# Four edits to the order and the blocks of a fused Hymba layer on one NeuronCore: norm matmuls moved, first weights in halves, bias matmuls moved, end in token blocks of 400, 400 and 256

## The chip, the core and the metric

The kernel runs on one core of one Trainium2 chip. The metric is the device time of one execution in microseconds (us); lower is better. Engines are named as in the profile: PE (TensorE matmul), PEld (its weight load), DVE (VectorE), ACT (ScalarE), POOL (GpSimd), SP (the queue that issues most transfers). Each engine runs its own instructions strictly in the order of the program that was built for it, and waits where an operand is not there yet.

## The reference, cut to what matters

One step of a hybrid streaming encoder: 16 meta tokens, 1024 prompt tokens and 32 sample tokens, 1072 columns in all, model width 1024.

```python
h = rmsnorm(x, norm_mix); z = h @ w_in          # 1024 -> 1792: GLU, q, k, v
a = silu(layernorm(depthwise_conv31(glu)))      # conv group
o = sliding-window attention with sinks and a relative-position bias
x = x + concat([a, o]) @ w_out
u = rmsnorm(x, norm_ffn) @ w_up                 # 1024 -> 2 * 2816
x = x + (silu(depthwise_conv3(gate)) * up) @ w_down
y = rmsnorm(x, norm_final)
```

The meta tokens give no output row of `y`, so the end of the program works on 1056 columns.

## The kernel before, in words

**Layout.** Features lie on the 128 partitions, tokens along the free axis; width 1024 is eight tiles `k` (or `m`) of 128. Almost every product is made three times for accuracy (`mm3`, lines 237 to 242): operands are split into a rounded part and a remainder (`hi`, `lo`), and PE adds hi·hi, lo·hi and hi·lo (lines 240, 241, 242). The split costs one ACT instruction (rounding) and one DVE instruction (subtraction) for every operand. A group below means all matmuls that fill one accumulator; with eight `k` it has 24.

**Order.** In most regions the order of PE (and of ACT and DVE in some) is the order in which the Python code is written (`manual_schedule`). The other engines' order is set by the builder's own scheduler. In the region of the first feed-forward groups (from line 1314) only PE is ordered by hand.

**Start.** PE first runs 18 dummy products (`warm`, line 292). Line 297 loads the weights of the first two output tiles (`raw`, 512 KB each) on SP and splits them; then `xT` comes in twelve pieces of two `k` each (line 299), for three token blocks of 336, 384 and 352 columns (`TB`). `gsplit` (line 273) makes `hi` on ACT and `lo` on DVE for every `k`; `sq_sum` (line 266) squares on ACT and adds up on DVE for the norm. The first PE groups (`START`) take two output tiles against block 0, `k` by `k`, then one tile each against blocks 1 and 2.

**A norm** (`rms_steps`, line 244) has three steps. One: PE sums the squares over partitions (`R<-ones`, line 252: per sub-block of up to 128 tokens one matmul with one column), DVE line 253, POOL line 254 (a power of -0.5) and DVE lines 255 to 257 (one Newton step). Two: ACT makes one diagonal matrix `diag` for each sub-block (line 260). Three: PE multiplies it by ones (`R<-diag`, line 263), which spreads the factors over all partitions. Each `next()` on the generator emits one step.

**Bias setup** (`bias_setup`, line 380) has five steps too; the fourth is two matmuls `nb` (line 424) that read tiles `acc<-ld` which came by DMA, the fifth is `sb` and `mb` (lines 436, 439). `BS` lists the group (input tile number, token block) after which each step is emitted.

**Feed-forward start** (lines 1314 to 1363). The norm of the last token block (`last_rms`, line 1316) is made between the groups of the first feed-forward tile: `group(f, u, p, c)` has 24 matmuls of 266 or 264 columns, u = 0 the gate half, u = 1 the up half. Beside them `t_stage` (line 1215) builds sums and differences of activation blocks for a Strassen-like scheme: ACT `hraw` (line 1224), four DVE operations (1226 to 1229), ACT `th` and DVE `tl` (`hilo`, lines 1135, 1136). `gate_done(0)` (line 1249) needs the finished norm; the weights of tile 1 are split into the buffers of tile 0 (`w_plain`, lines 1135 and 1136 again), the second set into the buffers that the four u = 1 groups free.

**End** (lines 1467 to 1512). The last six of 22 products of the down projection are done block by block in the order 384, 352, 320 columns (`EO`, `YB`). Each of eight `m` takes 18 matmuls, a DVE add into `x` (line 1498), a square on ACT and a sum on POOL. `final` makes the norm of a finished block while the next block's products run: eight DVE operations (line 1477), and stores `yT` on SP. After the third block this tail has nothing beside it.

Of the kernel before, what the change touches and what calls it, by code (L numbers as in the profile page):

```python
# [17 lines left out]
P = 128  # L18
# [42 lines left out]
SQP = (8, 8, 7)  # L61
SQG = (8, 8, 8)
FS = 1
EO = (1, 2, 0)
EM = 5
LNW = (4, 3, 9, 6, 11, 3, 11)
# [91 lines left out]
def body(nc, tc, cp, wp, xp, dp, io):  # L158
# [27 lines left out]
    nc.vector.memset(stat, 1.0)  # L186
    mhalf = cp.tile([P, 3], F32, tag="mhalf", name="mhalf")
    nc.vector.memset(mhalf, -0.5)
# [55 lines left out]
    def rms_steps(sums, c, div, R):  # L244
        parts = sums if isinstance(sums, list) else [sums]
        n = parts[0].shape[-1]
        subs = (0, P, n - P)
        ss = R[:, 400:403]
        v, t, r = (stat[:, c + 3 * i:c + 3 * i + 3] for i in range(3))
# [4 lines left out]
        nc.gpsimd.tensor_tensor(out=r, in0=v, in1=mhalf, op=ALU.pow)  # L254
# [4 lines left out]
        for i in range(3):  # L259
# [16 lines left out]

    diag = [cp.tile([P, P], F32, tag=f"diag{i}", name=f"diag{i}") for i in range(3)]

# [16 lines left out]
    for b, (t0, n) in enumerate(TB):  # L295
        if b == 0:
            pre = [wload(d.win[c].rearrange("p a b -> p (a b)")) for c in range(2)]
        for k in range(0, KD, 2):
            nc.sync.dma_start(X[b][:, k:k + 2, :], d.xT[:, k:k + 2, t0:t0 + n])
        if b == 0:  # L300
            nc.scalar.dma_start(ident, d.cst[:, 0, :])
# [818 lines left out]
    with tc.tile_pool(name="psB", bufs=1, space=PSUM, reuse_waits="tile") as pf:  # L1120
# [295 lines left out]

        def d_mm(ps, ci, w, b):
            t0, n = YB[b]
            f0, f1 = CHUNKS[ci]
# [25 lines left out]
        for i, (ci, m) in enumerate(order[:2 * KD]):  # L1445
# [4 lines left out]
            for b in (1, 2, 0):  # L1450
                ps = mmt()[:, :YB[b][1]]
                d_mm(ps, ci, w, b)
                if ci == 0:
# [12 lines left out]

        def final(pos, b, parts):
            t0, n = YB[b]
            rms = rms_steps(parts, 27 + (pos % 2) * 9, D, pf.tile([P, 512], F32, tag="nm", name="R", bufs=2))
# [5 lines left out]
            w = 2 if pos < 2 else 1  # L1475
            for k in range(KD):
                nc.vector.scalar_tensor_tensor(out=XY(b, k), in0=XY(b, k), scalar=pcol("g3", k), in1=R,  # L1477
                                               op0=ALU.mult, op1=ALU.mult)
                if (k + 1) % w == 0:
                    nc.sync.dma_start(d.yT[:, k + 1 - w:k + 1, t0 - NMETA:t0 - NMETA + n],  # L1480
                                      X[b][:, k + 1 - w:k + 1, t0 - OB[b][0]:])
                if k % 2:
                    yield

        scrs = [z[:, i:i + 384] for z in (rbg, gx0) for i in (0, 384)]
        fin = None
# [3 lines left out]
        ends[3] = d_load(2, 3)  # L1490
        for pos, b in enumerate(EO):
            n = YB[b][1]
            for m in range(KD):
                if not pos and m + 4 < KD:
                    ends[m + 4] = d_load(2, m + 4)
                ps = mmt()[:, :n]
                d_mm(ps, 2, ends[m], b)
                nc.vector.tensor_tensor(out=XY(b, m), in0=XY(b, m), in1=ps, op=ALU.add)
                if m == 0:
                    parts = [rb[b][:, :n]]  # L1500
                if m < SQP[pos]:
                    sq_sum(XY(b, m), rb[b][:, :n], scr(n), m, nc.gpsimd if m < SQG[pos] else nc.vector)
                else:
                    parts.append(scr(n))
                    nc.scalar.activation(parts[-1], XY(b, m), AF.Square)
# [4 lines left out]
            fin = final(pos, b, parts)  # L1510
        for _ in fin:
# [95 lines left out]
```

## Time and profile before

| what | us |
|---|---|
| three runs | 1096.98, 1099.25, 1099.38 |
| median of the runs | 1099.25 |
| the profiled execution, its own time | 1095.78 |
| its span, first to last instruction | 1093.7 |
| PE busy in the span | 1060.2 |

The profiled execution lies 3.5 us under the median of the three runs, so durations read from it are set against 1095.78, and a difference is then taken over to the median. From 376 to 1080 us PE has no idle time that the profile shows, with the exception of 0.02 us near 820. Its idle time lies in the first 9 us, in the attention stretch from 180 to 260 us, in single places between 300 and 376 us, and in the last 13 us.

### The profile page before, as it was taken

To read this page: it belongs to the slowest core of one execution; us is meant where nothing else is said; L and a number is where in the kernel's file an instruction comes from. 1 tells how busy PE (TensorE), PEld (TensorE's weight loads), DVE (VectorE), ACT (ScalarE), POOL (GpSimd) and SP (SyncE) were. 2 spreads that over 40 slices of the span, in tenths; PEclk is the share of its full clock that TensorE was granted. 3 is DMA by queue.
4 is the path that set the end of the run, shared out by engine and by line. 5 is a ranking of instruction groups with operands and counts; after the bars stand their busy time and mean duration, and the time that the engine had idled before them with its cause. 6 is when DMAs were issued, how large, how long until landed. Compare 5 with 4: busy or idle time off the path is not lost.

```text
span 1093.7 us, 18848 instructions
## 1 busy us (share of the span) xinstructions
PE 1060.2 (97%) x7547; PEld 1033.7 (95%) x7547; DVE 775.0 (71%) x1321; ACT 468.6 (43%) x990; POOL 138.3 (13%) x189
## 2 busy tenths in 40 slices
PE   8999999989999699999999999999999999999996
PEld 7989997758999699999999999999999999999996
DVE  7799999999887778777778778777777203322244
ACT  8522227996766754334334334334344213111211
POOL 1111000012334100000000000000001111000231
PEclk9999999999999899999999999999999999999997
DMA  7344331125853111221221221221266746121012
GB/s 263 80 108 100 83 94 40 39 59 82 159 147 124 50 60 59 97 80 60 92 86 59 86 91 60 82 94 60 79 236 202 184 90 159 58 63 59 15 58 101
DMA packets 45823, 103.76 MB, mean 95 GB/s; under 512 B 7840, under 2 KB 25496, under 8 KB 45736
## 3 DMA queue, kind: packets, MB, share of 16 engines
q1 hardware_dynamic: 35912, 84.46, 23.4%
q0 software_dynamic: 9536, 17.89, 9.9%
q8 instruction: 59, 0.97, 0.4%
q14 instruction: 28, 0.23, 0.1%
q10 hardware_dynamic: 288, 0.22, 0.1%
HBM read 72.41 MB, written 21.02 MB: 85 GB/s over the span
## 4 chain that ended last, share of the span: by engine, by line
PE 65%; ACT 2%; DVE 1%; issue 1%; POOL 0%; POOLq 0%; DVEq 0%; ACTq 0%
PE mm L1204 38%; PE mm L240 9%; PE mm L241 9%; PE mm L242 9%; ACT hraw L1224 1%; PE R L263 0%; POOL rb L271 0%; DVE x L1477 0%; ACT bh L274 0%; DVE tl L1136 0%; ACT th L1135 0%; ACT acc L270 0%; ACT diag L260 0%; DVE x L1082 0%; DVE traw L1226 0%
## 5 line engine op out<-in xcount | busy, mean ns | idle before, releaser
L357 DVE SCALAR_TENSOR_TENSOR acc<-glu,prm,acc 128x1090 f32<-128x1090 f32 (+3 forms) x180 | 168.0, 967 | 0.4
L1204 PE MATMUL mm<-bh,sl 128*128 128x266 f32 (+1 forms) x544 | 117.5, 285 | 0.0
L240 PE MATMUL mm<-hi,whi 128*128 128x352 f32 (+3 forms) x312 | 104.5, 335 | 2.0 <-ACT hi L274 2.0
L241 PE MATMUL mm<-lo,whi 128*128 128x352 f32 (+3 forms) x312 | 102.2, 327 | 0.7 <-DVE lo L275 0.7
L242 PE MATMUL mm<-hi,wlo 128*128 128x352 f32 (+3 forms) x312 | 101.8, 326 | 0.0
L1204 PEld LDWEIGHTS mm<-bh,sl 128*128 128x128 f32 x544 | 90.7, 189 | 0.0
L1204 PE MATMUL mm<-th,sl 128*128 128x264 f32 (+1 forms) x384 | 90.2, 285 | 0.0
L1204 PE MATMUL mm<-bl,sl 128*128 128x266 f32 (+1 forms) x296 | 84.5, 285 | 0.0
L1204 PE MATMUL mm<-bh,whi 128*128 128x266 f32 (+1 forms) x320 | 80.9, 285 | 0.0
L240 PE MATMUL mm<-bh,whi 128*128 128x266 f32 (+4 forms) x224 | 68.2, 304 | 0.0
L241 PE MATMUL mm<-bl,whi 128*128 128x266 f32 (+4 forms) x224 | 67.7, 302 | 0.0
L242 PE MATMUL mm<-bh,wlo 128*128 128x266 f32 (+4 forms) x224 | 67.7, 302 | 0.0
L1204 PEld LDWEIGHTS mm<-th,sl 128*128 128x128 f32 x384 | 66.2, 188 | 0.0
L1204 PE MATMUL mm<-th,wlo 128*128 128x266 f32 (+1 forms) x240 | 65.3, 285 | 0.0
L240 PEld LDWEIGHTS mm<-hi,whi 128*128 128x128 f32 x312 | 58.9, 189 | 3.3 <-ACT hi L274 2.2
L241 PEld LDWEIGHTS mm<-lo,whi 128*128 128x128 f32 x312 | 59.1, 189 | 2.2 <-DVE lo L275 1.9
L242 PEld LDWEIGHTS mm<-hi,wlo 128*128 128x128 f32 x312 | 59.0, 189 | 0.0
L1204 PEld LDWEIGHTS mm<-bh,whi 128*128 128x128 f32 x320 | 57.1, 189 | 0.0
L1204 PEld LDWEIGHTS mm<-bl,sl 128*128 128x128 f32 x296 | 55.8, 188 | 0.0
L1204 PE MATMUL mm<-bh,wlo 128*128 128x266 f32 (+1 forms) x208 | 51.7, 284 | 0.0
L1204 PE MATMUL mm<-th,rawr 128*128 128x266 f32 (+1 forms) x208 | 49.1, 285 | 0.0
L1204 PE MATMUL mm<-bh,rawr 128*128 128x266 f32 (+1 forms) x208 | 49.0, 285 | 0.0
(374 smaller groups left out, 3234.3 us busy)
## 6 DMA issues: line engine op xcount, KB each, us to landing
x<-wup SPq DMA_DIRECT2D x40, 512.0 KB, 3.9
wlo<-raw POOLq DMA_DIRECT2D x16, 512.0 KB, 4.5
raw<-wdn SPq DMA_DIRECT2D x16, 512.0 KB, 6.6
raw<-win SPq DMA_DIRECT2D x14, 512.0 KB, 3.4
yd<-x SPq DMA_DIRECT2D x12, 528.0 KB, 2.9
yd<-rb SPq DMA_DIRECT2D x10, 528.0 KB, 3.0
rb<-yd SPq DMA_DIRECT2D x8, 528.0 KB, 5.1
x<-yd SPq DMA_DIRECT2D x7, 528.0 KB, 5.6
```

The lines of the kernel that those rows point to most:

```text
L240: nc.tensor.matmul(ps, whi(k), xhi(k), start=first and i == 0, stop=False)
L241: nc.tensor.matmul(ps, whi(k), xlo(k), start=False, stop=False)
L242: nc.tensor.matmul(ps, wlo(k), xhi(k), start=False, stop=last and i == n - 1)
L357: nc.vector.scalar_tensor_tensor(out=a, in0=e[:, a0 + k:a1 + k], scalar=pcol("cw", p * CW + k), in1=a, op0=ALU.mult, op1=ALU.add)
L1204: nc.tensor.matmul(ps, w[:, j, :], x, start=first and j + i == 0, stop=j == 3 and i == 2, skip_group_check=True)
L1224: nc.scalar.activation(h[:, 2 * i * n + lo_:2 * i * n + hi_], src, AF.Copy, scale=pcol("g2", k))
```

## The change

1. `last_rms`: its first step is emitted after the second group of u = 0 (before: after the third), its second after the third (before: fourth), its third after the first group of u = 1 (before: at once after the fourth group of u = 0).
2. The first two weight tiles come in halves of four `k`, each of 256 KB, two halves ahead of `x` 0 to 3 and two ahead of `x` 4 to 7, and are split half by half.
3. `BS`: steps four and five of the bias setup are emitted one group later.
4. The end works on blocks of 400, 400 and 256 columns that no longer coincide with the stored blocks of `x`; an add, a square, a final multiplication or a store that crosses a border is done in two pieces. `rms_steps` takes as many sub-blocks as the width needs (four for 400, two for 256). All squares run on ACT and all sums but the last on POOL, as before.

```diff
-BS = ((1, 0), (1, 1), (1, 2), (2, 0))
+BS = ((1, 0), (1, 1), (2, 0), (2, 1))
-EO = (1, 2, 0)
+ENDN = 400
+ENDS = ((NMETA + 256, ENDN), (NMETA + 656, ENDN), (NMETA, 256))
...
-        subs = (0, P, n - P)
+        subs = list(range(0, n - P, P)) + [n - P]
...
-            pre = [wload(d.win[c].rearrange("p a b -> p (a b)")) for c in range(2)]
+            pre = [[wp.tile([P, 1024], F32 if t == "raw" else F32R, tag=t, name=t) for t in ("raw", "whi", "wlo")]
+                   for c in range(2)]
         for k in range(0, KD, 2):
+            if b == 0 and k % 4 == 0:
+                for c in range(2):
+                    raw, hi, lo = (z[:, k * P:k * P + 512] for z in pre[c])
+                    nc.sync.dma_start(raw, d.win[c, :, k:k + 4].rearrange("p a b -> p (a b)"))
+                    split(hi, lo, raw)
             nc.sync.dma_start(X[b][:, k:k + 2, :], d.xT[:, k:k + 2, t0:t0 + n])
...
             group(0, 0, i // 2, i % 2)
-            if i > 1:
+            if 0 < i < 3:
                 next(last_rms)
             next(t0s)
-        next(last_rms)
-        gate_done(0)
         w_plain(1, 0, *plain[:2])
         for i in range(4):
             group(0, 1, i // 2, i % 2)
+            if i == 0:
+                next(last_rms)
+                gate_done(0)
             next(t1s)
...
             for k in range(KD):
-                nc.vector.scalar_tensor_tensor(out=XY(b, k), in0=XY(b, k), scalar=pcol("g3", k), in1=R,
-                                               op0=ALU.mult, op1=ALU.mult)
+                for lo_, hi_, x in x_cols(k, t0, n):
+                    nc.vector.scalar_tensor_tensor(out=x, in0=x, scalar=pcol("g3", k), in1=R[:, lo_:hi_],
+                                                   op0=ALU.mult, op1=ALU.mult)
```

The order of DVE around the last block's norm (`stat` are the norm's small operations, `traw`, `rb`, `tl` and `t` belong to `t_stage`), before:

```order
L1227 TENSOR_TENSOR traw<-hraw_3618,traw 128x266
L1136 TENSOR_TENSOR tl_3611<-traw,th_3609 128x3x266
L1226 TENSOR_TENSOR traw<-hraw_3619 128x266
L1228 TENSOR_TENSOR traw<-hraw_3619 128x266
L1229 TENSOR_TENSOR rb<-hraw_3618,traw 128x266
L253 TENSOR_SCALAR stat<-R 128x3
L1227 TENSOR_TENSOR traw<-hraw_3619,traw 128x266
L1229 TENSOR_TENSOR rb<-hraw_3619,traw 128x266
L255 SCALAR_TENSOR_TENSOR stat<-stat 128x3
```

The same place of DVE after (line numbers of the changed kernel, up to eight away):

```order
L1234 TENSOR_TENSOR traw<-hraw_3625,traw 128x266
L1236 TENSOR_TENSOR rb<-hraw_3625,traw 128x266
L252 TENSOR_SCALAR stat<-R 128x3
L1143 TENSOR_TENSOR tl_3618<-traw,th_3616 128x3x266
L254 SCALAR_TENSOR_TENSOR stat<-stat 128x3
L1233 TENSOR_TENSOR traw<-hraw_3626 128x266
L1235 TENSOR_TENSOR traw<-hraw_3626 128x266
L255 TENSOR_TENSOR stat<-stat 128x3
L1234 TENSOR_TENSOR traw<-hraw_3626,traw 128x266
L256 SCALAR_TENSOR_TENSOR stat<-stat 128x3
L1236 TENSOR_TENSOR rb<-hraw_3626,traw 128x266
```

The first `stat` operation and one `rb` operation have moved ahead of a `tl` operation; what stands before them on DVE is the same.

The order of ACT at the same place, where the diagonal matrices are made, before:

```order
L1330 COPY gx_3613<-mm 128x264
L1224 ACTIVATE hraw_3618<-x_2244,prm 128x176
L1224 ACTIVATE hraw_3618<-x_2245,prm 128x352
L1135 CAST th_3609<-traw 128x3x266
L1224 ACTIVATE hraw_3619<-x_2244,prm 128x176
L1224 ACTIVATE hraw_3619<-x_2245,prm 128x352
L260 ACTIVATE diag_93<-ident,stat 128x128
```

And after:

```order
L1231 ACTIVATE hraw_3626<-x_2251,prm 128x176
L1231 ACTIVATE hraw_3626<-x_2252,prm 128x352
L1142 CAST th_3616<-traw 128x3x266
L259 ACTIVATE diag_93<-ident,stat 128x128
L259 ACTIVATE diag_94<-ident,stat 128x128
L259 ACTIVATE diag_95<-ident,stat 128x128
L1337 COPY gx_3620<-mm 128x264
```

One accumulator copy (`gx`) and two `hraw` operations that stood ahead of the `diag` operations now follow them; the `th` operation still stands ahead of them.

The order of ACT at the start of the program, after (before, one row `CAST whi<-raw 128x1024 x2` stood in the place of the first of these, and the second cast row was not there):

```order
L232 CAST whi<-raw 128x512 x2
L273 ACTIVATE hi_79<-xs_103,prm 128x336 x2
L267 ACTIVATE acc<-xs_103 128x336
L269 ACTIVATE sq<-xs_103 128x336
L273 ACTIVATE hi_79<-xs_103,prm 128x336 x2
L269 ACTIVATE sq<-xs_103 128x336 x2
L232 CAST whi<-raw 128x512 x2
L273 ACTIVATE hi_79<-xs_103,prm 128x336 x2
```

The second halves' casts stand between the pieces of `x`; on DVE the second halves' subtractions stand at the corresponding place.

## Rows read from the trace of the kernel before

**Rows 1.** The page, busy time, share of the span and instruction counts.

```profile
PE 1060.2 (97%) x7547; PEld 1033.7 (95%) x7547; DVE 775.0 (71%) x1321; ACT 468.6 (43%) x990; POOL 138.3 (13%) x189
```

**Rows 2.** Waits of PE, whole span: us in total, times, longest us.

```profile
PE R L263 <- ACT diag L260: 10.6, 2, 8.3
...
PE mm L240 <- ACT hi L274: 2.0, 1, 2.0
```

**Rows 3.** Timeline of PE, feed-forward start: start, us, what, [idle before <-releaser].

```profile
360.88 0.72 PE L252 MATMUL R<-ones,rb 128*128 128x1 f32 x6
...
364.35 0.28 PE L242 MATMUL mm<-bh,wlo 128*128 128x264 f32 x1
372.98 1.65 PE L263 MATMUL R<-diag,ones 128*128 128x128 f32 x6 [8.35 <-ACT diag L260]
374.28 0.57 PE L240 MATMUL mm<-bh,whi 128*128 128x266 f32 x1
...
392.94 0.28 PE L242 MATMUL mm<-bh,wlo 128*128 128x264 f32 x1
```

**Rows 4.** Timeline of DVE, the same stretch.

```profile
365.95 0.43 DVE L1227 TENSOR_TENSOR traw<-hraw,traw 128x266 f32<-128x266 f32 x1
367.49 0.99 DVE L1136 TENSOR_TENSOR tl<-traw,th 128x798 fp32r<-128x798 f32 x1 [1.12 <-ACT th L1135]
...
369.21 0.43 DVE L1229 TENSOR_TENSOR rb<-hraw,traw 128x266 f32<-128x266 f32 x1
369.56 0.15 DVE L253 TENSOR_SCALAR stat<-R 128x3 f32<-128x3 f32 x1
...
388.95 1.22 DVE L1136 TENSOR_TENSOR wlo<-raw,whi 128x1024 fp32r<-128x1024 f32 x1
```

**Rows 5.** Timeline of ACT, the same stretch.

```profile
370.97 0.84 ACT L1135 CAST th<-traw 128x798 fp32r<-128x798 f32 x1
372.54 0.97 ACT L260 ACTIVATE diag<-ident,stat 128x128 f32<-128x128 f32 x3
...
386.93 1.05 ACT L1135 CAST whi<-raw 128x1024 fp32r<-128x1024 f32 x1 [0.61 <-PE mm L241]
```

**Rows 6.** Timelines of SP, ACT, DVE and PE in the first 26 us.

```profile
8.04 0.37 SPq L299 DMA_DIRECT2D xs<-xT  x1
8.82 0.37 SPq L299 DMA_DIRECT2D xs<-xT  x1
...
6.49 1.04 ACT L209 CAST whi<-raw 128x1024 fp32r<-128x1024 f32 x1 [1.02 <-DMA raw<-win]
8.12 1.04 ACT L274 ACTIVATE hi<-xs,prm 128x336 fp32r<-128x336 f32 x2 [0.58 <-DMA xs<-xT]
...
8.72 1.05 DVE L275 SCALAR_TENSOR_TENSOR lo<-xs,prm,hi 128x336 fp32r<-128x336 f32 x2
...
25.03 0.43 PE L241 MATMUL o<-lo,whi 128*128 128x352 f32 x1 [0.21 <-DVE lo L275]
```

**Rows 7.** Timeline of PE around the bias matmuls.

```profile
65.01 1.74 PE L424 MATMUL nb<-acc,glu 128*128 128x448 f32 x4 [0.96 <-DMA acc<-ld]
...
70.30 0.76 PE L436 MATMUL sb<-acc,glu 128*128 128x354 f32 x2
```

**Rows 8.** Timelines of PE and DVE after the last product, and one group of DVE operations by form.

```profile
1082.20 0.36 PE L252 MATMUL R<-ones,rb 128*128 128x1 f32 x2
1082.43 0.46 PE L252 MATMUL R<-ones,rbg 128*128 128x1 f32 x2
1085.16 1.65 PE L263 MATMUL R<-diag,ones 128*128 128x128 f32 x6 [2.28 <-ACT diag L260]
...
1086.85 3.76 DVE L1477 SCALAR_TENSOR_TENSOR x<-x,prm,R 128x320 f32<-128x320 f32 x8 [2.24 <-PE R L263]
...
L1477 DVE SCALAR_TENSOR_TENSOR x<-x,prm,R 128x384 f32<-128x384 f32 x8 | 4.5, 608 | 0.0
```

**Rows 9.** Transfers, whole span: issue, engine, count, KB each, median us to landing.

```profile
cap<-glu SPq DMA_DIRECT2D x4, 15.0 KB, 2.9
```

More of the change, by code (lines that the diff above doesn't have):

```diff
@@ L186, in body @@
     nc.vector.memset(stat, 1.0)
-    mhalf = cp.tile([P, 3], F32, tag="mhalf", name="mhalf")
+    mhalf = cp.tile([P, 4], F32, tag="mhalf", name="mhalf")
     nc.vector.memset(mhalf, -0.5)
@@ L246, in rms_steps @@
         n = parts[0].shape[-1]
-        subs = (0, P, n - P)
-        ss = R[:, 400:403]
-        v, t, r = (stat[:, c + 3 * i:c + 3 * i + 3] for i in range(3))
+        subs = list(range(0, n - P, P)) + [n - P]
+        ns = len(subs)
+        ss = R[:, 400:400 + ns]
+        v, t, r = (stat[:, c + ns * i:c + ns * i + ns] for i in range(3))
         for i, at in enumerate(subs):
@@ L258, in rms_steps @@
         yield
-        for i in range(3):
+        for i in range(ns):
             nc.scalar.activation(diag[i], ident, AF.Copy, scale=r[:, i:i + 1])
@@ L275, in gsplit @@
         nc.vector.scalar_tensor_tensor(out=lo, in0=x, scalar=g, in1=hi.bitcast(F32), op0=ALU.mult, op1=ALU.subtract)
-    diag = [cp.tile([P, P], F32, tag=f"diag{i}", name=f"diag{i}") for i in range(3)]
+    diag = [cp.tile([P, P], F32, tag=f"diag{i}", name=f"diag{i}") for i in range(4)]
     cPS = tc.tile_pool(name="psA", bufs=1, space=PSUM, reuse_waits="tile")
@@ L296, in body @@
         if b == 0:
-            pre = [wload(d.win[c].rearrange("p a b -> p (a b)")) for c in range(2)]
+            pre = [[wp.tile([P, 1024], F32 if t == "raw" else F32R, tag=t, name=t) for t in ("raw", "whi", "wlo")]
+                   for c in range(2)]
         for k in range(0, KD, 2):
+            if b == 0 and k % 4 == 0:
[3 more added lines that the diff above has]
+                    split(hi, lo, raw)
             nc.sync.dma_start(X[b][:, k:k + 2, :], d.xT[:, k:k + 2, t0:t0 + n])
+        if b == 0:
+            pre = [z[1:] for z in pre]
         if b == 0:
@@ L1415, in d_load, with d_mm @@
             return kv(hi[:, :w]), kv(lo[:, :w])
-        def d_mm(ps, ci, w, b):
-            t0, n = YB[b]
+        def d_mm(ps, ci, w, t0, n):
             f0, f1 = CHUNKS[ci]
@@ L1451, in body @@
                 ps = mmt()[:, :YB[b][1]]
-                d_mm(ps, ci, w, b)
+                d_mm(ps, ci, w, *YB[b])
                 if ci == 0:
@@ L1465, in body, with final @@
         region.__exit__(None, None, None)
-        def final(pos, b, parts):
-            t0, n = YB[b]
-            rms = rms_steps(parts, 27 + (pos % 2) * 9, D, pf.tile([P, 512], F32, tag="nm", name="R", bufs=2))
+        def final(pos, parts):
+            t0, n = ENDS[pos]
+            rms = rms_steps(parts, (pos % 2) * 12, D, pf.tile([P, 512], F32, tag="nm", name="R", bufs=2))
             for _ in range(2):
@@ L1490, in body @@
         ends[3] = d_load(2, 3)
-        for pos, b in enumerate(EO):
-            n = YB[b][1]
+        for pos, (t0, n) in enumerate(ENDS):
+            last = pos + 1 == len(ENDS)
             for m in range(KD):
@@ L1496, in body @@
                 ps = mmt()[:, :n]
-                d_mm(ps, 2, ends[m], b)
-                nc.vector.tensor_tensor(out=XY(b, m), in0=XY(b, m), in1=ps, op=ALU.add)
+                d_mm(ps, 2, ends[m], t0, n)
                 if m == 0:
[L1500 to L1505, printed above, removed]
+                    parts = [rbt[:, t0:t0 + n]]
+                to = parts[0] if m == 0 else scr(n)
+                for lo_, hi_, x in x_cols(m, t0, n):
+                    nc.vector.tensor_tensor(out=x, in0=x, in1=ps[:, lo_:hi_], op=ALU.add)
+                    nc.scalar.activation(to[:, lo_:hi_], x, AF.Square)
+                if 0 < m < KD - last:
+                    nc.gpsimd.tensor_tensor(out=parts[0], in0=parts[0], in1=to, op=ALU.add)
+                elif m:
+                    parts.append(to)
                 if pos and m >= FS:
@@ L1509, in body @@
                 pass
-            fin = final(pos, b, parts)
+            fin = final(pos, parts)
         for _ in fin:
```

13 lines of the change are left out of this document (5 added, 8 removed).

## The prediction, made before the run

> **What bounds the kernel now.** Read the page's busy shares first: PE works 97% of the span [rows 1]. So a saving counts only where PE stands still, or where the program ends without it. The waits of PE name those places [rows 2]: 10.6 us in two waits for the diagonal matrices of a norm, 8.3 of them in one, and 2.0 us for the first `hi` operand. The timeline adds 0.96 us before the bias matmuls [rows 7]. The large wait stands in the feed-forward start: PE ends its fourth group at 364.5 and starts `R<-diag` at 372.98 [rows 3]. The second wait for `diag`, 2.28 us, is in the tail, which no product covers: DVE's last eight multiplications start at 1086.85 and end at 1090.61 [rows 8], and the span ends at 1093.7.
>
> **Edit 1, the norm in the feed-forward start.** Why was `diag` so late? PE had its column sums at 360.88 plus 0.72 [rows 3], but DVE took them up only at 369.56, behind a `tl` and an `rb` operation [rows 4]; ACT then ran a cast at 370.97 before `diag` at 372.54 [rows 5]. So the delay lies in two queues, not in the matmuls' place alone. The edit moves three things. The column sums come one group earlier on PE, which gains nothing by itself, since DVE was the late one. DVE's first operation moves from behind the `tl` of 367.49 to behind an `rb` that can follow the operation of 365.95 at once [rows 4]: about 366.8, 2.8 us earlier. But on ACT `diag` still stands behind the cast of 370.97; only a copy and two `hraw` operations move behind it. That cast is fed by the same alternation of DVE and ACT as before, so `diag` starts at about 371.6 (370.97 and 0.84, less a copy moved behind) instead of 372.54, and PE gets it at about 372.1. On the other side PE now runs one more group first. A group lasts 3.0 us (from the end of the sums, about 361.5, to 364.35 and 0.12), so PE arrives at about 367.9, some 0.4 of it a wait for the sum on POOL. The wait shrinks from 8.35 to about 4.2, it does not vanish.
>
> If PE then ran free, the third product of the third group of tile 1, which stands at 392.94 [rows 3], would come at 372.1 + (392.94 - 372.98) - 3.0 = 389.1: a gain of 3.9. What is late next is its operand: this product is the first that reads the second `wlo` of tile 1, which DVE made at 388.95 to 390.15 [rows 4]. I walked the 32 DVE rows between with the durations of before and with ACT's copies of the norm now behind one copy more: the `wlo` starts at about 388.5, nearly where it was, since DVE's amount of work up to it is the same. So PE waits there for some 0.6 us, and the place gives 392.94 - 389.7 = **3.2**. Bounds: if the gate chain, which starts only after the norm's copies, slips by 2 us more, 1.2; if DVE is 1 us ahead of my walk, 3.9. PE also ran at half speed after the long wait: 0.57 for the first product at 374.28 against 0.28 [rows 3]. If the shorter wait spares PE that slow time, about 1.5 us, PE only arrives earlier at the same `wlo`; at most, with DVE ahead as well, 5.4.
>
> **Edit 2, the weights in halves.** The first `hi` waited for the first piece of `x`, which landed at 8.04 (SP's issue is released by it; the piece after came 0.78 later) [rows 6]. 512 KB less stand in front of it. At the rate between these two pieces of 336 KB (0.43 MB per us) that is 1.2 us; at the rate between the second weight tile, landed by 6.49, and the first piece, 2.4 us. PE's dummy products end 2.04 us before its first real one, so PE itself could use up to 2.0. But the work of splitting is not less, it now stands between the pieces of `x`: on ACT two casts of half of 1.04 each [rows 6], on DVE two subtractions of half of 1.22 (the same operation as at 388.95 [rows 4]). DVE is what PE follows there: `lo` starts at 8.72, and PE waits for a `lo` as late as 25.03 [rows 6]. DVE's stream starts earlier by 1.2 to 2.1 and has 1.2 to 1.3 more to do from there on, so the stretch ends 0 to 0.9 earlier. I take **0.5**, near the middle; PE then waits 1 us or more at the fifth `k` where it waited at the first. A page of the Trainium skill speaks against this edit: "DMA: Bandwidth & Descriptors", section "Bandwidth", advises transfers of 1 MiB or more, since each carries a fixed share. By its fixed share of about 2.0 us per transfer, if none overlapped, the first piece of `x` would land later than now and the edit would cost about 0.7. The pieces landing 0.78 apart [rows 6] show that transfers overlap here, so the sum does not use that.
>
> **Edit 3, the bias matmuls.** PE waits 0.96 before `nb` for a transfer, and the `sb` group follows one group, 4 us, later without a wait [rows 7]. One group later the transfer has 3.7 us more; ACT's copies and DVE's bias operations have no reader for tens of us. Gain **0.95**, bounds 0.3 (if DVE, which is nearly full there, gives half of it back later) and 1.2.
>
> **Edit 4, the end.** The columns are 1056 in both, the products 144 for each block in both, so the products cost the same. The four-part norms of the two wide blocks add one column-sum pair and one `R<-diag` pair to PE each, amid its products: four pairs at up to 0.24 (0.72 for three [rows 3]), taken as 0.2, costs **0.8**. The split adds, squares and stores on DVE, ACT and SP lie beside 18 products of over 0.1 us each and cost nothing unless DVE fills up: in the third block eight small pieces come on top of work that left DVE idle most of the time. The tail shrinks from 320 columns in three sub-blocks to 256 in two: two column-sum pairs, 0.23 (from 1082.20 to 1082.43) each, 0.46; one pair of `R<-diag`, 1.65/3 = 0.55; eight multiplications, each shorter by the slope between 608 ns at 384 columns and 543 at 320 (4.5/8 against 3.76/8 gives the same, 1 ns a column), 0.065 times 8 = 0.52; add and square together 0.12. Sum **1.65**. Bounds 1.0 (if SP's issues of about 0.4 each bind in place of DVE) and 2.1 (if the smaller stores land faster too).
>
> **Sum.** 3.2 + 0.5 + 0.95 - 0.8 + 1.65 = 5.5. Against the profiled execution, 1095.78 - 5.5 = 1090.3; the median of the runs lies 3.5 above that execution, so 1099.25 - 5.5 = **1093.7**.
>
> **Rivals.**
> (a) *The wait moves down the DVE queue.* The norm's copies stand later on ACT, so the gate chain on DVE slips and `wlo` with it; edit 1 gives 1.2 or less, the sum 2.0 to 3.4, time about 1096.4. For it: DVE is in order and PE already reads `wlo` 2.8 us after it is made [rows 3, 4], so every us beyond that is a wait. Against it: DVE's total work up to that row is unchanged. Chance 0.2.
> (b) *PE runs free.* DVE is ahead of my walk and the clock stays up: edit 1 gives 5 and the sum is 7.3, time about 1091.9. Chance 0.15.
> (c) *The early gains are lost* in the attention stretch where PE waits for other engines: edits 2 and 3 give nothing, 1099.25 - 4.05 = 1095.2. Against it: DVE, which is full there, itself waits for PE before, so it would start that stretch earlier. Chance 0.07.
> (d) *Slower: the narrow stores hold the end.* The stores of 64 and 48 columns, eight of them, go on SP's queue ahead of the last block's eight. The nearest row, a store of 15 KB in short runs, lands in 2.9 us [rows 9]. The last narrow store is issued about 5 us before the first final one. It must take more than 5 + 5.5 = 10.5 us to make the program slower at all, and 14 for 0.3%. Chance 0.03. The same page's section "Specifications" asks for 512 bytes or more in one run, and below that an extra read; these runs have 256 and 192 bytes, and no run here shows a store of this form yet.
> The forecast as summed keeps 0.55.
>
> **Chances.** About 0.3% (3.3 us) is what a measurement of this kernel can tell from no change. Faster by more than that: the forecast, (b), (c), and a quarter of (a): 0.82. Within it: the rest of (a), 0.15. Slower: (d), 0.03. The range 1090.0 to 1097.0 takes in (a) to (c) with their bounds, with the spread of the three runs on either side.
>
> **What would show it.** In the changed profile: the wait before `R<-diag` near 370 at about 4 us (right) or near 8 (wrong), with `diag` on ACT behind the cast; a short new wait near 388 for `wlo` (a longer one is rival (a), none is (b)); the wait for the first `hi` gone and one of 1 us or more at the fifth `k`; no wait before `nb`; six `R<-diag` records in the tail reduced to four, and the time from the last product to the end at about 11.7 instead of 13.3. The prediction is wrong if DVE's `wlo` comes after 392 or if the last stores land more than 4 us after the last multiplication.

## The result: 0.67% faster than before, 1090.7 us

The changed kernel took 1090.66 us, the median of four runs (1090.1 to 1091.2); the kernel before took 1098.12 in four runs beside it. The ratio is 0.9933, with an interval of 0.9915 to 0.9951. When both were run again (below), the ratio was 0.9944 (0.9931 to 0.9956), with the kernel before at 1096.64. The forecast was 1093.7 in a range of 1090.0 to 1097.0, and a gain of 5.5 us. The whole gain is 7.5 us in the first comparison and 6.1 in the second, so its size was near, but not for all of the reasons given: one of the four edits costs time.

The page of the changed kernel and its waits of PE (us in total, times, longest), for [rows 1] and [rows 2]:

```profile
PE 1062.2 (98%) x7549; PEld 1035.2 (95%) x7549; DVE 777.3 (71%) x1355; ACT 471.9 (43%) x1009; POOL 144.9 (13%) x189
```

```profile
PE R L262 <- ACT diag L259: 5.1, 2, 3.0
...
PE mm L238 <- DVE x L1089: 1.9, 2, 1.6
PE mm L239 <- DVE lo L274: 1.5, 3, 0.7
```

The two waits for `diag` fell from 10.6 to 5.1, and the large one among them from 8.3 to 3.0. The wait for the first `hi` (2.0) and the one before `nb` (0.96) are gone. In their place stand longer waits for `lo` at the start (1.5 for 0.7; 0.65 of it at the fifth `k`, where 1 us or more was forecast) and for a DVE result near 313 us (two waits, 1.9 for 1.3).

The feed-forward start after, for [rows 3 to 5]: timelines of PE, then DVE, then ACT (start, us, what, [idle before <-releaser]).

```profile
367.93 0.28 PE L240 MATMUL mm<-bh,wlo 128*128 128x266 f32 x1
371.19 1.65 PE L262 MATMUL R<-diag,ones 128*128 128x128 f32 x6 [2.98 <-ACT diag L259]
372.49 0.57 PE L238 MATMUL mm<-bh,whi 128*128 128x266 f32 x1
...
388.27 0.29 PE L239 MATMUL mm<-bl,whi 128*128 128x264 f32 x1
388.68 0.39 PE L240 MATMUL mm<-bh,wlo 128*128 128x264 f32 x1
```

```profile
366.93 0.15 DVE L252 TENSOR_SCALAR stat<-R 128x3 f32<-128x3 f32 x1
...
386.23 1.25 DVE L1268 TENSOR_TENSOR x<-x,rbg 128x1058 f32<-128x1058 f32 x1
387.40 1.22 DVE L1143 TENSOR_TENSOR wlo<-raw,whi 128x1024 fp32r<-128x1024 f32 x1
```

```profile
369.99 0.84 ACT L1142 CAST th<-traw 128x798 fp32r<-128x798 f32 x1
370.74 0.98 ACT L259 ACTIVATE diag<-ident,stat 128x128 f32<-128x128 f32 x3
```

PE runs one group more before the norm, waits 2.98 in place of 8.35, and reads the second `wlo` of tile 1 at 388.68 in place of 392.94. Between 388.27 and 388.68 a product's spacing of 0.12 is missed by 0.29: PE came to that operand just ahead of it. So the operand named in the prediction is what is late next, and the place gave 392.94 - 388.68 = 4.26, not 3.2.

### The profile page after: what moved, and what is told of

The parts are those of the page before. It is cut to its first block, busy times and chain, and to the rows that moved or that the text cites. A ratio compares the mean times of both kernels' runs of the same rounds, so it can differ in the third digit from the quotient of the medians.

```text
span 1089.4 us, 18949 instructions
## 1 busy us (share of the span) xinstructions
PE 1062.2 (98%) x7549; PEld 1035.2 (95%) x7549; DVE 777.3 (71%) x1355; ACT 471.9 (43%) x1009; POOL 144.9 (13%) x189
## 4 chain that ended last, share of the span: by engine, by line
PE 63%; DVE 3%; ACT 2%; issue 1%; POOL 0%; POOLq 0%; DVEq 0%; ACTq 0%
PE mm L1211 38%; PE mm L240 8%; PE mm L238 8%; PE mm L239 8%; ACT hraw L1231 1%; DVE tl L1143 1%; ACT bh L273 0%; ACT th L1142 0%; PE R L262 0%; DVE x L1485 0%; POOL rb L270 0%; ACT acc L269 0%; DVE traw L1233 0%; DVE wlo L1143 0%; DVE x L1264 0%
```

## Where the two kernels part: four places in the traces

This table, read from the timelines of PE, shows when PE stands at the same point of the program: the start of the second column sums in the first 31 us, the column sums of the first block after attention, the first product of the stage that follows the feed-forward start (`mm<-bh,sl`), the column sums just behind the last product, and the span.

| profiled kernel | column sums 2 | after attention | next stage | last product | span |
|---|---|---|---|---|---|
| before | 28.99 | 325.72 | 410.40 | 1080.21 | 1093.7 |
| changed | 29.58 | 325.80 | 406.21 | 1076.98 | 1089.4 |
| changed, run again | 30.34 | 325.39 | 406.52 | 1077.30 | 1089.7 |
| edit 1 alone | 29.02 | 325.43 | 405.85 | 1075.66 | 1089.0 |
| edit 2 alone | 30.23 | 329.43 | 415.35 | 1085.16 | 1098.9 |
| edit 3 alone | 29.14 | 324.42 | 409.92 | 1079.73 | 1093.1 |
| edit 4 alone | 28.60 | 325.20 | 410.27 | 1081.05 | 1092.9 |
| changed without edit 2 | 28.83 | 323.86 | 404.29 | 1075.07 | 1086.7 |

Between the two profiled executions, then: nothing up to 325 us (-0.08), 4.27 in the feed-forward start, -0.96 before the last product, 1.07 behind it. Together 4.3. Two questions follow: where the gains of edits 2 and 3 went, and why the medians lie further apart than the profiles.

## Experiments: each edit alone on the kernel before

The kernel before took 1096.34 us here (22 runs, 1095.02 to 1099.11).

**Edit 1, the norm.**

```diff
-            if i > 1:
+            if 0 < i < 3:
                 next(last_rms)
...
             group(0, 1, i // 2, i % 2)
+            if i == 0:
+                next(last_rms)
+                gate_done(0)
```

> The kernel before with edit 1 alone. Theory A (the forecast): PE leaves the norm about 4 us earlier and then stands for the second wlo of tile 1; gain 3.2 us, bounds 1.2 to 3.9, ratio about 0.9971. Theory B (the trace of the changed kernel): DVE makes this wlo at 387.4 instead of 388.95, since the norm's operations and the casts moved up on DVE and ACT alike; PE reaches it only 0.3 us too early; gain 4.3 us, ratio about 0.9961. In the trace both want one wait of about 3 us before the diagonal products near 371; A wants the wlo of tile 1 after 388, B at about 387.4.

1091.78 us, ratio 0.9957 (0.9944 to 0.9969). PE reads the `wlo` at 388.31, the stage from the column sums after attention to `mm<-bh,sl` is 4.26 shorter than before. Theory B in its numbers; the mechanism is the one that both share.

**Edit 2, weights in halves.**

```diff
+            if b == 0 and k % 4 == 0:
+                for c in range(2):
+                    raw, hi, lo = (z[:, k * P:k * P + 512] for z in pre[c])
+                    nc.sync.dma_start(raw, d.win[c, :, k:k + 4].rearrange("p a b -> p (a b)"))
+                    split(hi, lo, raw)
```

> The kernel before with edit 2 alone. Theory A (the forecast): 0.5 us faster, bounds 0 to 0.9. Theory B (the trace of the changed kernel, where the products of the third token block and the first norm's diagonal products at 42 us stand 0.5 to 0.6 us later than before): the edit makes the start about 0.6 us slower, because the added halves of casts and subtractions stand between the x pieces on the engines that bound this stretch; and since attention from 180 us on absorbs shifts of this size, the whole is 0 to 0.6 us slower.

1100.53 us, ratio 1.0032 (1.0020 to 1.0045): slower than either theory had it. The trace shows 1.24 lost in the first 31 us, where theory B had 0.6, and then something new at the bias matmuls. Timelines of SP and PE, and the clock (the columns of the last row: stretch, length, busy us and instructions of PE, PEld, DVE, ACT and POOL, then PEclk, DMA share, GB/s):

```profile
61.00 1.80 SPq L411 DMA_DIRECT2D acc<-ld  x1
```

```profile
67.70 2.67 PE L432 MATMUL nb<-acc,glu 128*128 128x448 f32 x4 [2.42 <-DMA acc<-ld]
...
70.45 0.48 PE L241 MATMUL mm<-lo,whi 128*128 128x336 f32 x1
```

```profile
68.00:72.00 4.00, 4.00 (x12) 2.70 (x11) 3.72 (x3) 3.09 (x19) 0.00 (x0) 0.57 0.10 13
```

One issue of the bias transfers occupied SP for 1.80 us, where such issues take about 0.6. The transfer landed later, PE waited 2.42 in place of 0.96 [rows 7], and the granted clock, 1.0 before this wait (2.4 GHz), was 0.57 behind it, near the lower of its two levels (0.50, 1.2 GHz); products took 0.48 in place of 0.32. From `nb` to the first product of 384 columns PE needed 7.64 us, before 6.02. So this one late transfer cost 1.46 as a wait and 1.62 at the lower clock; 2.47 of the two are left at the column sums after attention. The long issue is not tied to the halves alone: it stands in five of fourteen profiles (1.80 to 2.00), three with halves and two without.

**Edit 3, the bias matmuls.**

```diff
-BS = ((1, 0), (1, 1), (1, 2), (2, 0))
+BS = ((1, 0), (1, 1), (2, 0), (2, 1))
```

> The kernel before with edit 3 alone. Theory A (the forecast): the wait of 0.96 us before the bias matmuls goes and the program ends 0.95 us earlier, bounds 0.3 to 1.2. Theory B: the 0.96 us go at 65 us, but the attention stretch, where DVE has no idle time, starts no earlier, and PE waits longer behind it (in the changed kernel the wait at 313 us grew from 0.99 to 1.65): no change at the end. Theory C: in other executions of the kernel before the transfer lands later than in the profiled one, which makes its times spread over 3 us; then this edit alone gives 1 to 3 us and its own runs spread less.

1094.92 us, ratio 0.9983 (0.9974 to 0.9992), eleven runs between 1093.49 and 1095.12. Theory B is out: the gain is not absorbed. From the second column sums to those after attention PE takes 295.28 us, before 296.73, so 1.45 is won. In the changed kernel's rows the matmuls now start without a wait, which they also do where the issue took 1.8 to 2.0 us:

```profile
68.04 0.31 PE L240 MATMUL mm<-hi,wlo 128*128 128x336 f32 x1
68.19 1.66 PE L431 MATMUL nb<-acc,glu 128*128 128x448 f32 x4
```

The runs spread over 1.6 us, those of the kernel before over 4.1. That fits theory C, but none of the longer executions of the kernel before was profiled, so that a late bias transfer makes them longer is argued from edit 2's trace and not shown. (The list of PE's idle places given with the profile before leaves this one at 65 us out.)

**Edit 4, the end.**

```diff
-EO = (1, 2, 0)
+ENDN = 400
+ENDS = ((NMETA + 256, ENDN), (NMETA + 656, ENDN), (NMETA, 256))
```

> The kernel before with edit 4 alone. Theory A (the forecast): 0.8 us lost on the extra norm products and 1.65 us won in the tail, 0.85 us faster in all, bounds 0.2 to 1.3. Theory B (the two traces): 0.96 us lost before the last product and 1.1 us won behind it, 0.1 us faster, which is no difference to be measured. In the trace the time from the last product to the end is 12.4 us under B and 11.7 under A.

1095.97 us, ratio 0.9998 (0.9989 to 1.0006). It can't be told from no change, nor from the 0.85 of the forecast. In the trace it loses 0.97 between `mm<-bh,sl` and the last product (669.81 before, 670.78 here), and the rest behind it takes 11.85 in place of 13.49.

**What the table shows beside the edits.** From the column sums after attention to `mm<-bh,sl` the kernel before took 84.68, and with edits 2, 3 and 4 alone 85.92, 85.50 and 85.07, though none of these edits touches that stage. All four have the wait of 8.4 us before `R<-diag`; the difference arises behind it, from `R<-diag` to `mm<-bh,sl` (37.42, and 38.63, 38.22 and 37.81), in the order in which the clock came back. The stretch of 2 to 4 us behind the start of `R<-diag`, the kernel before and then edit 2:

```profile
374.98:376.98 2.00, 2.00 (x14) 2.00 (x14) 1.69 (x2) 2.00 (x6) 0.18 (x1) 0.75 0.36 117
```

```profile
378.72:380.72 2.00, 2.00 (x11) 2.00 (x10) 1.68 (x2) 2.00 (x6) 0.19 (x1) 0.50 0.40 102
```

Edits 4 and 3 have 0.56 and 0.50 there; from 4 to 6 us behind it edit 3 has 0.80 and edit 2 has 0.58, the other two 1.00. So the profiled execution of the kernel before is the shortest of four at this place, by up to 1.2 us, and the table's gain of edit 1 is the smallest of four (4.26, against the others 4.7 to 5.5). This is a likely reason, though no run shows it by itself, why the medians lie further apart than the profiles.

## Experiments: the whole change, and parts of it undone

The kernel before took 1096.64 us here (nine runs).

**The changed kernel again**, no edit.

> The changed kernel once more, beside many runs of the kernel before on the same chip. The traces of the single edits add up, by the place where PE stands in each: norm 4.3 us, bias and halves together 0 (1.3 won, 1.4 lost), end 0.2 to 0.7; together 4.5 to 5, and on top of it what the kernel before loses in those executions in which the bias transfer lands late. Theory A (the sum of the forecast): 5.5 us faster, ratio 0.9950. Theory B (the first comparison, 0.9933, stands): 7.4 us. Theory C: 5 us, ratio 0.9955, since the four runs of the kernel before in that comparison were high.

1090.58 us, ratio 0.9944 (0.9931 to 0.9956): 6.1 us. That is between theories A (0.9950) and B (0.9933), and the interval holds all three, so the times don't decide. A wait of 1.12 for the first `hi` is left in this profile.

**Edit 2 undone.**

```diff
-            pre = [[wp.tile([P, 1024], F32 if t == "raw" else F32R, tag=t, name=t) for t in ("raw", "whi", "wlo")]
-                   for c in range(2)]
+            pre = [wload(d.win[c].rearrange("p a b -> p (a b)")) for c in range(2)]
```

> The changed kernel with edit 2 undone (weights whole, ahead of x). Theory A (the forecast): 0.5 us slower than the changed kernel. Theory B (the traces: with the bias edit alone the norm of the first block after attention starts at 324.4, with halves as well at 325.8): 1.4 us faster than the changed kernel. The trace decides by the same place: about 324.4 under B, 326.3 under A.

1088.72 us (1088.52 to 1089.01), ratio 0.9926 (0.9913 to 0.9940). All five runs lie below all five of the changed kernel beside it (1090.26 to 1091.52): 1.9 us faster. Theory B holds: the place after attention stands at 323.86. **This version is better than both kernels.**

Why do the halves cost? The first rows are the changed kernel's ACT, then its DVE, for [rows 6]; the last is DVE of the kernel before.

```profile
6.75 1.04 ACT L273 ACTIVATE hi<-xs,prm 128x336 fp32r<-128x336 f32 x2 [0.69 <-DMA xs<-xT]
...
10.13 1.12 ACT L232 CAST whi<-raw 128x512 fp32r<-128x512 f32 x2
```

```profile
11.04 1.29 DVE L233 TENSOR_TENSOR wlo<-raw,whi 128x512 fp32r<-128x512 f32 x2
...
25.01 0.55 DVE L270 TENSOR_TENSOR acc<-acc,sq 128x384 f32<-128x384 f32 x1
25.48 2.57 DVE L274 SCALAR_TENSOR_TENSOR lo<-xs,prm,hi 128x352 fp32r<-128x352 f32 x5
```

```profile
24.40 3.06 DVE L275 SCALAR_TENSOR_TENSOR lo<-xs,prm,hi 128x352 fp32r<-128x352 f32 x6
```

The first piece of `x` does come earlier: ACT starts on it at 6.75 to 7.50 in four profiles with halves, at 7.72 to 8.26 in ten without. Then 1.12 of casts and 1.29 of subtractions stand in the stretch where both engines have next to no idle time, and the scheduler puts one more square sum ahead of the last `lo` operations, which end at 28.05 in place of 27.46. PE, which follows `lo`, ends the stretch later. The sum can be made on DVE: from the first `lo` to the end of the last it takes 20.69 (7.36 to 28.05), before 18.74 (8.72 to 27.46), so 1.95 more, of which 1.29 are the subtractions and 0.47 the square sum (25.01 to 25.48). The start 1.36 earlier gives back less than that. In the second profile of the changed kernel the stretch is 20.69 again, but it starts only 0.61 earlier (8.11), and `lo` ends at 28.80.

**The second block's square sums on POOL.**

```diff
-            sq_sum(X[b][:, k, :], parts[k % NSUM], sq, k // NSUM)
+            sq_sum(X[b][:, k, :], parts[k % NSUM], sq, k // NSUM, nc.gpsimd if b == 1 else None)
```

> The changed kernel with its halves, and the sums of squares of the second token block (384 columns) on POOL in place of DVE. This asks why the halves cost time. Theory A: because two of these sums now stand ahead of the lo operations of the third block on DVE (they end at 28.05 against 27.46), and PE follows lo; then with the sums off DVE the lo operations end at 27.5 or earlier, PE's waits for lo of the third block vanish, and the second norm's column sums at 29.6 come at 29.0 or earlier: the kernel is 0.6 us or more faster than the changed one. Theory B: ACT, busy without a gap from 6.8 to 30, is the bound and the halves add 1.1 us of casts to it; then lo comes no earlier than its hi and the gain is under 0.3 us.

1090.78 us, ratio 0.9948 (0.9935 to 0.9960): no gain, and not for theory B's reason. The second column sums came at 31.80, 2.2 later than in the changed kernel. DVE by form, 14 to 31 us (count, busy us, mean ns of one), the changed kernel first, then this one:

```profile
L274 DVE SCALAR_TENSOR_TENSOR lo<-xs,prm,hi 128x384 fp32r<-128x384 f32 x8 | 4.8, 611 | 0.0
```

```profile
L274 DVE SCALAR_TENSOR_TENSOR lo<-xs,prm,hi 128x384 fp32r<-128x384 f32 x8 | 6.5, 829 | 0.0
...
L254 DVE SCALAR_TENSOR_TENSOR stat<-stat 128x3 f32<-128x3 f32 x1 | 0.8, 832 | 0.3 <-POOL stat L253 0.3
```

While POOL adds, DVE's operations take longer, a tiny one 0.83 in place of 0.16. So this run can't answer its question, how the cost of edit 2 divides between the added work and the sum that moved ahead; only the reading of DVE's rows above does. The Trainium skill ("GPSIMD Engine Reference", section "Specifications") says that POOL shares its memory interfaces with DVE and names DVE instructions with two inputs from that memory among those that contend; these rows agree.

The run was useful elsewhere. Its feed-forward start came out in another order by the scheduler's doing: `wlo` at 386.38, 27.09 after the norm's column sums, where the changed kernel has 28.90; and the stage from the column sums to `mm<-bh,sl` took 45.89 in place of 47.71. Both are 1.8 shorter.

**The third norm step one group later still** (weights whole).

```diff
-            if i == 0:
+            if i == 1:
                 next(last_rms)
                 gate_done(0)
```

> The changed kernel with weights whole (as in the run before this one) and the third norm step one group later still, after the second group of u = 1. In the changed kernel PE waits 2.98 us for the diagonal matrices and 0.3 us, 17 us later, for the second wlo of tile 1. Theory A (the forecast's: the wlo is next late): the 2.98 us go, but the gate chain starts up to 3 us later, the wlo comes no earlier, and PE waits there 2.7 us or more instead: no gain against the kernel of the run before, 0 to 1 us slower. Theory B (PE was the cause of the late wlo, since it frees the buffer of whi): whi and wlo come earlier with PE, and the gain is 1.5 to 3 us.

1091.65 us, ratio 0.9952 (0.9940 to 0.9965): 2.9 slower than with the step where the change put it. The wait for `diag` is gone, and PE waits for both weight halves of tile 1:

```profile
384.25 0.39 PE L238 MATMUL mm<-bh,whi 128*128 128x264 f32 x1 [2.40 <-ACT whi L1134]
...
386.95 0.59 PE L240 MATMUL mm<-bh,wlo 128*128 128x264 f32 x1 [2.20 <-DVE wlo L1135]
```

Theory A in kind: the wait moves down, it does not go. The stage is 2.6 longer, more than theory A had, and most of that is the clock. The product that reads the `wlo` starts 30.54 behind the column sums, 0.37 later than in the version with whole weights (30.17); from there to `mm<-bh,sl` PE takes 19.73 in place of 17.54, at a granted clock of 0.50 from 386 to 390 us and 0.55 up to 392, where that version has 1.00. So here the clock fell behind the two waits at the weights, and nothing covers that loss.

## Experiments: the clock, and edit 4 on a steadier base

All four have weights whole; the kernel before took 1096.65 us here (nine runs).

**Six products put on PE during the wait for `diag`.**

```diff
         yield
+        for _ in range(keep):
+            nc.tensor.matmul(R[:, 0:P], ones, ones, start=True, stop=True)
         for i, at in enumerate(subs):
```

> The changed kernel with weights whole, and six products of the ones tile with itself put on PE just ahead of the diagonal products of the last block's norm, where PE otherwise stands idle for 2.97 us and then runs at half clock for some 3 us. Their result is overwritten. This asks what the clock costs there and who is late behind it. Theory A (the second wlo of tile 1 is next late): the diagonal products take 0.83 us in place of 1.32 and the products behind them 0.12 each in place of 0.22, PE gains 1.2 to 1.6 us up to the wlo and gives it back there as a wait: gain 0 to 0.4 us against the kernel without the six. Theory B (wlo moves with PE): gain 1.2 us or more, first product of the next stage (mm<-bh,sl) at 403.0 in place of 404.3.

1091.80 us, ratio 0.9952 (0.9940 to 0.9965). The clock in the stretch of 370 to 374 is 1.00 (0.58 with whole weights and no such products, 0.50 in the kernel before), PE is earlier by what the clock gave, and waits for the weights again. The last two rows show the clock behind these waits:

```profile
385.52 0.39 PE L238 MATMUL mm<-bh,whi 128*128 128x264 f32 x1 [0.99 <-ACT whi L1136]
...
387.07 0.39 PE L240 MATMUL mm<-bh,wlo 128*128 128x264 f32 x1 [1.04 <-DVE wlo L1137]
```

```profile
388.00:390.00 2.00, 2.00 (x11) 2.00 (x10) 2.00 (x4) 0.15 (x1) 2.00 (x1) 0.50 0.01 4
390.00:392.00 2.00, 2.00 (x15) 2.00 (x14) 2.00 (x4) 0.70 (x1) 1.03 (x1) 0.73 0.04 15
```

Nothing is won, as theory A said; the stage is even 2.3 longer. Of this, 0.75 is the order's: the insertion also made the scheduler put the gate chain later on DVE, and the `wlo` starts 29.65 behind the column sums in place of 28.90. The other 1.54 is the clock's, lost behind the new waits (19.08 from the `wlo`'s product to `mm<-bh,sl`, in place of 17.54).

**Seven products ahead of the tail's `R<-diag`**, the same line with `keep` at 7 for the last block.

> The changed kernel with weights whole, and seven products of the ones tile with itself on PE just ahead of the last diagonal products, in the tail. Theory A: the tail's four diagonal products run at full clock, 0.55 to 0.6 us in place of 1.18, nothing stands between them and the end that could take it back, gain 0.5 us. Theory B: the clock has already fallen during the column sums and does not rise in this time, so the seven take 0.57 us each, 4 us, longer than the wait of 2.1 us, and the kernel is 1 to 2 us slower.

1089.15 us, ratio 0.9931 (0.9917 to 0.9944): no gain, and by the times no loss that can be told (0.9926 without the seven). The clock was 0.50 from 1078 to 1080, the seven took 3.1 us in place of a wait of 2.1, and DVE's last multiplications started 6.17 after the last product in place of 4.94. In the traces this is theory B: the part behind the last product takes 12.88, without the seven 11.63.

**Both insertions.**

> Both insertions of the two runs before this one. Expected: the sum of the two; under theory A of both 0.5 to 0.9 us faster than the changed kernel with weights whole (1088.7 in the session before), under B of both about as fast as that.

1091.19 us, ratio 0.9951 (0.9939 to 0.9964): nothing won. The order of DVE is that of the first insertion, and so are the waits at the weights (0.80 and 1.04), but here the clock stayed at 1.00 behind them and the stage takes 48.27, only 0.56 longer than without. The rest of the loss is in the tail, 13.16 in place of 11.63.

**Edits 1 and 3 alone** (edits 2 and 4 undone).

```diff
-ENDN = 400
-ENDS = ((NMETA + 256, ENDN), (NMETA + 656, ENDN), (NMETA, 256))
+EO = (1, 2, 0)
```

> The kernel before with edits 1 and 3 (norm and bias): the changed kernel with edits 2 and 4 undone. Edit 4 alone against the kernel before gave 0.2 us with an interval of 0.7 us below to 1.2 us above; on this base the times spread less. Theory A (the forecast): 0.85 us slower than the same with edit 4 (1088.7 in the session before). Theory B (the trace of edit 4 alone: 0.97 lost to the norm products, 1.4 won up to the last store, the landing of the stores varying by 0.5): 0.2 to 0.7 us slower.

1089.78 us, ratio 0.9938 (0.9926 to 0.9951). The intervals of this and of the kernel with edit 4 (0.9926) overlap, so the times alone don't separate them. In the traces the last product comes 669.80 after `mm<-bh,sl` here and 670.78 with edit 4, the remainder takes 13.34 here and 11.63 with it: 0.98 lost, 1.71 won, 0.73 in all.

This run also shows, by chance, what the clock is worth at the norm. Its order is that of the changed kernel there, and so is its wait of 2.98, but its clock stayed up. The stretch of 370 to 374 of the changed kernel, the same of this one, and this one's wait at the `wlo`:

```profile
370.00:374.00 4.00, 2.81 (x13) 2.81 (x14) 2.83 (x6) 4.00 (x11) 0.19 (x1) 0.65 0.00 0
```

```profile
370.00:374.00 4.00, 4.00 (x35) 4.00 (x33) 2.82 (x6) 4.00 (x11) 0.19 (x1) 1.00 0.35 108
```

```profile
387.12 0.39 PE L242 MATMUL mm<-bh,wlo 128*128 128x264 f32 x1 [1.55 <-DVE wlo L1136]
```

PE gained 1.26 from the clock and waited 1.55 in place of 0.29. The stage took 47.72, the changed kernel's 47.71. Edit 1 alone and the kernel with whole weights have 47.72 and 47.71 as well, at clocks of 0.57 and 0.58, and in all of them the `wlo` starts 28.90 or 28.91 after the column sums. So DVE's second `wlo` sets the end of this stage, as long as the clock is full behind it (17.53 or 17.54 from its product to `mm<-bh,sl`). One profile shows the edge of that: in the changed kernel run again the clock was 0.50 in this stretch, PE came to the `wlo` without a wait, and the stage took 48.39.

## Why the prediction was right, and where it was not

**What bounds the kernel: right.** The gains came from PE's waits and from the tail.

**Edit 1: mechanism right, size low.** Forecast 3.2, bounds 1.2 to 3.9, measured 4.26 (and 4.7 to 5.5 against the kernels with edits 2, 3 or 4 alone, for their clock). The wait at `R<-diag` was forecast at 4.2 and is 2.98, since `diag` starts at 370.74 and not at 371.6: the `th` cast ahead of it also moved, from 370.97 to 369.99. The larger part of the miss is the `wlo`: walked at 388.5, it starts at 387.40. The step that failed is "DVE's amount of work up to it is the same", from which I took that its time was the same. In the kernel before, DVE stood idle inside that stretch, waiting for the gate's result from ACT:

```profile
385.54 1.26 DVE L1261 TENSOR_TENSOR x<-x,rbg 128x1058 f32<-128x1058 f32 x1 [1.06 <-ACT x L1260]
```

After, the same operation (386.23) has other work in front of it and no wait. The order could have told this. Rival (a), the wait down the queue, did not come with this change, but it is what one group more does (the norm later still) and what a raised clock does. Rival (b), PE free, is out: a faster PE only waits longer there.

**Edit 2: wrong in sign.** Forecast 0.5 faster, bounds 0 to 0.9; with edit 3 in place it costs 1.9 us, without it 3.5 (ratio 1.0032). The failed step is the sum on DVE, a stream that "starts earlier by 1.2 to 2.1" and has 1.2 to 1.3 more to do: in the four profiles with halves the first `lo` started 0.6 to 1.4 earlier than in the kernel before (7.36 to 8.11 against 8.72), and in the changed kernel DVE had 1.95 more to do. The scheduler's other order of the square sums was left out of the sum. Without edit 3 a lower clock behind a late bias transfer came on top; whether the later start makes that transfer late more often is not shown. What the sentence on the Trainium skill ("DMA: Bandwidth & Descriptors", section "Bandwidth") would have given, a loss of 0.7 by a later first piece of `x`, has the sign of the result, but not its cause: the piece came earlier, as the row on it had said. The 0.7 also compares a sum without overlap after the edit with a landing measured with overlap before it; two transfers stand ahead of that piece in both kernels, so a fixed share for each can't make it later. (The 2.0 stands on the same page in the section "Anatomy of one DMA — SWDGE (gpsimd) path", for transfers issued by GpSimd; these are issued by SP.)

**Edit 3: right, larger.** Forecast 0.95, at most 1.2; 1.45 in the traces and 0.17% (0.08 to 0.26%) in the times. Only 0.96 of it is the wait seen in the profile. What was missed is that this wait differs from profile to profile (0.93 to 1.24 in three, 2.42 in the one with edit 2 alone), and that behind the wait of 2.42 the clock fell.

**Rival (c) is out.** I gave 0.07 to a loss of early gains in attention. Among kernels with edit 3 the time from the second column sums to those after attention is 294.4 to 295.4 in all but one of them, whether they start early or late. That one is the first profile of the changed kernel (296.2), with a longer wait at 313 us (1.65 where the others with edit 3 have at most 0.84); why it came so late is not explained. So the zero at 325 us is no absorption: edit 3 won, edit 2 lost.

**Edit 4: places right, size only in part.** Forecast 0.85 (1.65 won, 0.8 lost). On the base of edits 1 and 3 the traces give 1.71 won and 0.98 lost, but in the two profiles of the changed kernel itself only 1.07 and 1.09 won against the kernel before, and 0.96 and 0.97 lost: 0.1 in all. Over the profiles with a last block of 256 (without the two that have seven products in the tail) the part behind the last product takes 11.6 to 12.5, in five of seven 12.3 or more, where 11.7 was forecast. The times never told the gain from zero. The rows for [rows 8] in the first profile of the changed kernel are at the long end, with `R<-diag` at 1.18 (0.78 in the version without edit 2):

```profile
1081.12 1.18 PE L262 MATMUL R<-diag,ones 128*128 128x128 f32 x4 [2.12 <-ACT diag L259]
```

```profile
1082.34 3.22 DVE L1485 SCALAR_TENSOR_TENSOR x<-x,prm,R 128x256 f32<-128x256 f32 x8 [1.77 <-PE R L262]
1082.84 3.78 SPq L1489 DMA_DIRECT2D yT<-x  x8
```

The same two groups with a last block of 320, from the run with edits 1 and 3 alone:

```profile
1081.01 3.75 DVE L1478 SCALAR_TENSOR_TENSOR x<-x,prm,R 128x320 f32<-128x320 f32 x8 [2.23 <-PE R L263]
1081.58 3.80 SPq L1481 DMA_DIRECT2D yT<-x  x8
```

The term that failed is that of the eight multiplications. They are 0.53 shorter, as summed (0.52), but the eight stores behind them are issued on SP 0.48 apart in both kernels, and from the first multiplication to the end of the last issue it takes 4.28 with 256 columns and 4.37 with 320: 0.09 won. Over all profiles it is 4.27 to 4.30 and 4.36 to 4.38. So the forecast's own lower bound, 1.0 if SP's issues bind, describes what happened. Where 1.7 was reached all the same, the column sums came up 0.74 shorter (0.46 and 0.12 forecast) and `R<-diag` ran at a higher clock, so that size is in part luck. The slope that the sum rests on, 1 ns a column, is right, but the second source that was named for it gives 1.4 (4.5/8 against 3.76/8).

Rival (d), the narrow stores, did not come: pieces of 64 and 48 columns landed in 1.8 and 1.6 us by the page of transfers.

**The sum and the median.** By pairs of profiles the four edits add up to 4.3 - 1.5 + 1.45 and 0.1 to 0.7, that is 4.3 to 5.0, near the forecast's 5.5 by two errors that cancel (edit 1 low, edit 2 of the wrong sign); this is luck. Between the medians 6.1 to 7.5 were measured. The profiled executions lie 4.3 to 4.6 apart (1095.78 against 1091.52 and 1091.20): the one of the kernel before is 0.6 to 0.9 shorter than its later medians, those of the changed kernel are 0.9 and 0.5 longer than theirs. The forecast time was 3 us high for another reason: I took the offset of 3.5 between the profiled run and the median of three as fixed. In 40 further runs the kernel before had medians of 1096.3 to 1096.7. Set against 1096.5, a gain of 5.5 gives 1091.0, and 1090.6 was measured.

## What to carry to other kernels

- A wait on PE that several engines feed is worth what the next late operand leaves of it. Find that operand and walk its engine in the new order, idle gaps included: here one DVE subtraction set the end of a stage to 0.01 us, at three different clocks of PE. And walk the queue behind the last step as well: at the end of this kernel SP's issues took back what shorter multiplications had won.
- Splitting a load to start earlier pays only if the engine that then works is idle. Where ACT and DVE are full, the work that moves into their full stretch and a shifted schedule cost more than the earlier byte gives.
- A wait for a transfer that shows as 0.96 in one profile was 2.4 in the profile of another version, with a clock loss behind it. Slack there was worth more than the profiled wait. Runs that spread may be a hint to such a wait, but here also to the clock behind a long wait elsewhere.

## What was not expected of the hardware

- The same wait of 2.98 us on PE left the granted clock at 0.50 to 0.65 in the stretch from 370 to 374 us in five profiles, and at 1.00 in a sixth. Shorter waits at that place (1.21 with the sums on POOL, 1.64 behind the six products) left it at 1.00. Two waits 1.6 us apart at the weights of tile 1 (0.99 and 1.04) left it at 0.50 in one profile, and nearly the same two (0.80 and 1.04) at 1.00 in another.
- An issue on SP's queue that takes 0.6 us took 1.8 to 2.0 in five of fourteen profiles, always the second of the bias transfers `acc<-ld`, with the same code around it.
- POOL's additions slowed DVE's operations of 128x384 from 611 to 829 ns on average, and a three-column one from 0.16 to 0.83 us.
